# Band attention in a two-block layer: keys of two blocks laid over one another on 128 places, values held as weights, and its steps in other slots

## The chip, the cores and the metric

One core of a Trainium2 chip runs the whole program in one launch. The metric is the device time in microseconds (us) of one execution, as a median of several runs. Engines are named as the profile names them: PE multiplies matrices, PEld is PE's loading of weights, DVE and ACT work element by element, POOL does a few small powers, and SP issues the transfers (DMA).

## The reference, cut to what matters

The program computes two blocks on 512 tokens of width 1024. The change concerns one part of the second block, an attention in which a query sees its own place and the 127 before it, with a learnt "sink" in every denominator:

```
s = einsum('bnqgrd,bnkgd->bngrqk', qb, kband) / sqrt(64)    # kband: the block before and the own block, 256 keys
valid = (rel >= 0) & (rel < 128) & (kpos >= 0)              # rel = query place - key place
s = where(valid, s, -inf)
m = maximum(max(s, -1), sk)
p = exp(s - m);  p = p / (sum(p, -1) + exp(sk - m))
o = einsum('bngrqk,bnkgd->bnqgrd', p, vband)
o_at = rms_norm(o.reshape(B, S, 512), attn_norm_g)
y = concatenate([h_ml, o_at], -1) @ w_out                   # h_ml: the mLSTM branch
x = x + g1 * rms_norm(y, post_mix_g)
```

There are 4 blocks of 128 queries, 8 query heads of width 64, and 2 key heads that serve 4 query heads each. A query at place q of its block sees the keys k > q of the block before and the keys k <= q of its own block: 128 keys in all, one for every k.

## The kernel before, in words

Every large product is made in three PE passes of a format with half the cost of full float32 (a high and a low part of each operand; the trace names operands hh, hl, whi, wlo). ACT makes the high part of a weight tile (whi), DVE the low part (wlo, line 243), and PE takes them in lines 273 (tile ga), 311 and 351 (gb) and 1480 (go). Smaller products, attention among them, are made in full float32, which PE runs as two instructions for one product.

In the second block's mixer PE goes through sixteen slots of about 24 such products each (`fill_items`: queries and keys of the mLSTM, its values, its output gates). After each slot a string names the steps that are put there (`MIX_SLOTS`): R are rotations of queries and keys, A the attention, M the mLSTM, G its gates, W weights of the output projection. `A23` is step 3 of query block 2. A scheduler then fixes the order of each engine's instructions, and every engine works through its own in that order: a PE instruction that waits holds all that stand behind it. PSUM tiles of the attention come from one ring of four (`PS`, tag "ps").

The attention of one query block (`att_stages`, lines 1295 to 1356) has six steps. Steps 0 and 1, one for each half of the heads: two mask products (line 1306, tile sps) put minus 1e30 at forbidden places of two PSUM tiles, four score products (line 1310) are added, DVE takes the maxima over 256 places (line 1313), ACT takes the exponentials out of PSUM and sums them (line 1322). Steps 2 and 3: PE transposes the 128x256 exponentials of each head in two pieces (line 1334, tile ptps), ACT copies them (line 1336). In step 3 the products with the values follow (line 1343, tile ops): the transposed exponentials are the weights, 64 columns of values move; DVE divides by the denominators (line 1346). Step 4 norms over the 512 features of a token (lines 1350 to 1352). Step 5 transposes the result (line 1362, tile tps) and splits it into high and low (lines 388 and 389, tiles ath and atl), ready to be the weights of the output projection (line 1480). Query block 0 has one key block, so its tiles have 128 places instead of 256.

Of the kernel before, what the change touches and what calls it, by code (L numbers as in the profile page):

```python
# [20 lines left out]
C_ID, C_TRI, C_STR, C_LAST, C_CNT, C_COS, C_SIN, C_NEG, C_ATT = (  # L21
    0, 128, 256, 384, 512, 576, 704, 832, 960)
C_W = 1216
# [3 lines left out]
def hybrid_kernel(  # L27
# [46 lines left out]
    # ---------------------------------------------------------------- constants  # L74
# [7 lines left out]
    def stage(parts):  # L82
        raw = small("colraw", [P, P])
        o = 0
        for a in parts:
            dma(out=raw[o:o + a.shape[0]], in_=a)
            o += a.shape[0]
        return raw, o
# [52 lines left out]
    # ---------------------------------------------------------------- adaLN modulation  # L141
# [3 lines left out]
    def ada_steps(ci, col):  # L145
        """steps that sum the products of the 128-column pieces col and col + 1 of w_ada over their k-tiles."""
# [12 lines left out]
    def ada_sum(ci, col, accs):  # L159
        """the sums over partitions of four pieces, as columns."""  # L160
# [16 lines left out]
    def pump():  # L177
        """half a piece of the modulation for every pump_rate[0] tiles of weights."""
# [32 lines left out]
    def cols_to_dram(name, col):  # L211
        """[P, n] columns -> n rows in DRAM."""
# [9 lines left out]
    def rows_bcast(name, dr, r0):  # L222
        """four rows of 128 from r0 on, the same in every partition."""
# [4 lines left out]
    def cols_to_rows(name, col):  # L228
        """[P, 8] columns -> two [P, 512] tiles with the vector in every row, by way of DRAM."""
# [8 lines left out]
    # ---------------------------------------------------------------- products  # L238
# [7 lines left out]
    def split_w(parts, kt=8):  # L246
        """weights [kt * 128, 256] (in column parts) -> per k-tile (hi, lo)."""
# [29 lines left out]
    def load_b(wmat, cols, k0):  # L277
        """two k-tiles of the columns [(first, number)] of wmat."""
# [8 lines left out]
    def keep(raw):  # L287
        """weights split into tiles that stay."""
# [129 lines left out]
    def h_tile(xh, j, p, ts, gc, bc, on_act=False, bank=PS):  # L418
        """features j of the tokens ts: transposed, scaled, shifted and split into p."""
# [14 lines left out]
    def first_tiles(ws, acts, between=None):  # L434
        """products of the first two 256-column weights, by token halves."""
# [8 lines left out]
    def conv(ps, name, cols, taps, b):  # L444
        """depthwise causal convolution of a [features, tokens] product; cols[k] are [P, 1]."""
# [7 lines left out]
    def silu2(u):  # L453
        """silu(2u), in place."""
# [4 lines left out]
    def log1p_exp_negabs(y, n, name):  # L459
        """log(1 + exp(-|y|)) of [P, n] with the relative accuracy of float32."""  # L460
# [15 lines left out]
    # ================================================================ block 1: mixer  # L476
# [68 lines left out]
    # parameters of the convolution  # L545
# [30 lines left out]
    # time steps: the k-tiles in four column groups of the tensor engine, summed with the transposition  # L576
# [15 lines left out]
    def xbc_items(g):  # L592
        """closures that add the convolved tiles of group g to XBC[g]."""
# [19 lines left out]
    # pool branch  # L613
# [25 lines left out]
    for q in (3, 2, 1, 0):  # L639
# [4 lines left out]
    # remaining parameters  # L644
    colF = columns("colF", stage([rows(a_) for a_ in (
        norm_mlp_w, pre_mix_g_2, pre_ffn_g_2, ssd_norm_w, pool_scale, attn_norm_g_2, post_mix_g_2, post_ffn_g_2)]
        + [ml_norm_g_2[0]]))
# [28 lines left out]
    ones_r = const("ones_r", [P, P], F32R)  # L676
    V.tensor_copy(out=ones_r, in_=ones)
    ident_r = const("ident_r", [P, P], F32R)
    V.tensor_copy(out=ident_r, in_=ident)
    masks = U("masks")[:, 0:3 * P]  # L680
    dma(out=masks, in_=consts[:, C_NEG:C_W])
    masks_r = const("masks_r", [P, 3 * P], F32R)
    V.tensor_copy(out=masks_r, in_=masks)
    neg_r, att_r = masks_r[:, 0:P], masks_r[:, P:]
# [27 lines left out]
    # time steps  # L712
# [47 lines left out]
    # state-space branch, a group of eight heads at a time  # L760
# [3 lines left out]
    def ssd_decay(g, cc, st):  # L764
        """what chunk cc of group g needs besides the state: scaled inputs, decayed scores, decayed C."""
# [54 lines left out]
    def ssd_out(g, cc, st):  # L820
        """the outputs of chunk cc of group g and the state after it."""
# [32 lines left out]
    def rms_stages(tiles, eps, wcol, name, res):  # L854
        """tiles [features, tokens] -> normed over all their features, scaled by wcol, split, added to res."""
# [43 lines left out]
    def branch_items(g):  # L899
        """the groups g - 1 and g."""  # L900
# [35 lines left out]
    def weave(stages, items):  # L936
        """emits the stages with the items [(cost, step)] spread evenly between them."""
# [11 lines left out]
    def take(items, share):  # L949
        """the leading items that make up a share of the cost."""  # L950
# [96 lines left out]
    # ================================================================ block 1: MLP  # L1047
# [95 lines left out]
    # ================================================================ block 2: mixer  # L1143
# [25 lines left out]
    # gates of the mLSTM  # L1169
# [58 lines left out]
    # queries and keys of the mLSTM, values and output gates  # L1228
# [24 lines left out]
    # sliding-window attention  # L1253
# [39 lines left out]
    AT = [None] * NCH  # L1293

    def att_stages(b):
# [4 lines left out]
        mx, nm, es, den = (small(n, [P, 8]) for n in ("amx", "anm", "aes", "aden"))  # L1300
        sm = []
        for hq in range(2):
            pse = [PS("sps") for _ in range(2)]
            p3s = [p_[:, 0:2 * nk].rearrange("p (h k) -> p h k", k=nk) for p_ in pse]
            for p3 in p3s:
                PE.matmul(p3, lhsT=ident_r, rhs=mask, start=True, stop=False)
            for i in range(2):
                hp = hq * 2 + i
                for r_, p3 in enumerate(p3s):
                    PE.matmul(p3[:, i], lhsT=QT[b][r_ * 64:(r_ + 1) * 64, hp * P:(hp + 1) * P],  # L1310
                              rhs=KT[hq][r_ * 64:(r_ + 1) * 64, k0:k0 + nk], start=False, stop=i == 1)
            for r_, p3 in enumerate(p3s):
                V.tensor_reduce(out=mx[:, hq * 4 + r_:hq * 4 + 4:2], in_=p3, axis=AX.X, op=ALU.max)
# [4 lines left out]
            u = [U("sm") for _ in range(2)]  # L1318
            for i in range(2):
                for r_ in range(2):  # L1320
                    h = hq * 4 + i * 2 + r_
                    act(out=u[r_][:, i * nk:(i + 1) * nk], in_=pse[r_][:, i * nk:(i + 1) * nk], func=AF.Exp, scale=0.125,
                        bias=nm[:, h:h + 1], accum_out=den[:, h:h + 1])
                    sm.append(u[r_][:, i * nk:(i + 1) * nk])
            yield
        act(out=es, in_=es, func=AF.Exp)
# [371 lines left out]
```

## Time and profile before

| | us |
|---|---|
| median of 3 runs | 1637.94 (1637.54 to 1638.12) |
| profiled execution: span from first to last instruction | 1635.9 |
| what lies around the span, median less span | 2.0 |
| PE busy in the span | 1605.5 |
| DVE busy in the span | 1069.6 |
| ACT busy in the span | 721.2 |

For the profiled execution the profile gives its span alone; its own time is therefore taken as the span and the 2.0 us. Attention runs from about 1085 us to 1186 us of the span. In lists of instructions a line of the profile gives the kernel's line, the engine, the operation, the tile written, the tiles read, and shapes as partitions x elements. The duration of a PE instruction includes its way through the array, so durations overlap: what one costs is read from start to start, or from the chain of waits, where a piece is counted once.

### The profile page before, as it was taken

Reading aid. Unit: us, or ns where it says so; the run is one execution under the profiler, and the core shown is the slowest. Engines: PE = TensorE matmul, PEld = TensorE weight load, DVE = VectorE, ACT = ScalarE, POOL = GpSimd, SP = SyncE. Lnnn points to the kernel's source line nnn. Section 1 sums busy time; section 2 is a strip of 40 time slices with the busy share of each in tenths; the row PEclk is TensorE's granted clock in tenths of the full one; section 3 lists DMA queues with packets and bytes.
Section 4 is the critical chain, followed back from the end, with each engine's and each line's share of the span. In section 5 each row is a group of like instructions: output and inputs, shape, how many; then the busy total and the mean of one; then the engine's idle time right before and its main releaser. Section 6 shows DMA issues by size and latency. Waiting matters only on the chain.

```text
span 1635.9 us, 21014 instructions
## 1 busy us (share of the span) xinstructions
PE 1605.5 (98%) x7942; PEld 1293.6 (79%) x7942; DVE 1069.6 (65%) x1944; ACT 721.2 (44%) x1279; POOL 28.1 (2%) x46
## 2 busy tenths in 40 slices
PE   5999999999999999999999999999999999999998
PEld 3778777777877878877877788878888888888886
DVE  6686898889676676875267654584576756245644
ACT  3543665555454333533123333646555544144421
POOL 0000000000000000000000000000001000000000
PEclk9999999999999999999999999999999999999999
DMA  9632544454544444565246571132232333332321
GB/s 284 185 104 66 174 142 142 130 160 132 158 129 142 129 140 144 167 201 185 91 143 194 181 242 27 53 93 62 72 105 71 90 91 103 91 103 82 99 90 52
DMA packets 206762, 206.52 MB, mean 126 GB/s; under 512 B 11397, under 2 KB 184645, under 8 KB 206661
## 3 DMA queue, kind: packets, MB, share of 16 engines
q1 hardware_dynamic: 206661, 205.19, 40.6%
q8 instruction: 62, 1.02, 0.3%
q14 instruction: 39, 0.32, 0.1%
HBM read 202.96 MB, written 2.19 MB: 125 GB/s over the span
## 4 chain that ended last, share of the span: by engine, by line
PE 93%; DVE 2%; DMA 2%; ACT 1%; issue 1%; POOL 0%; SPq 0%; DVEq 0%; POOLq 0%; ACTq 0%
PE ga L273 54%; PE gb L351 21%; PE gb L311 5%; PE go L1480 2%; PE ga L543 2%; DMA wraw<-in_w_ada_dram 1%; PE yps L831 1%; PE ops L1343 1%; PE stps L840 1%; PE nps L423 1%; PE sps L1310 1%; PE yps L836 1%; PE adaps L163 0%; PE xtps L792 0%; PE ptps L1334 0%
## 5 line engine op out<-in xcount | busy, mean ns | idle before, releaser
L243 DVE TENSOR_TENSOR wlo<-wraw,whi 128x1024 fp32r<-128x1024 f32 (+3 forms) x249 | 298.0, 1198 | 256.3 <-ACT whi L242 256.0
L273 PE MATMUL ga<-hh,whi 128*128 128x512 f32 (+1 forms) x1200 | 465.2, 390 | 0.3 <-ACT hh L430 0.3
L273 PE MATMUL ga<-hl,whi 128*128 128x512 f32 (+1 forms) x1200 | 459.2, 384 | 3.0 <-DVE hl L432 2.9
L273 PE MATMUL ga<-hh,wlo 128*128 128x512 f32 (+1 forms) x1200 | 458.0, 382 | 0.0
L242 ACT ACTIVATE whi<-wraw 128x1024 fp32r<-128x1024 f32 (+3 forms) x249 | 257.8, 1036 | 341.2 <-PE ga L273 152.1
L273 PEld LDWEIGHTS ga<-hl,whi 128*128 128x128 f32 x1200 | 226.0, 189 | 52.4 <-DVE hl L432 3.9
L273 PEld LDWEIGHTS ga<-hh,whi 128*128 128x128 f32 x1200 | 224.6, 188 | 53.2 <-issue 6.4
L273 PEld LDWEIGHTS ga<-hh,wlo 128*128 128x128 f32 x1200 | 226.1, 189 | 47.1 <-issue 0.3
L156 DVE SCALAR_TENSOR_TENSOR adacc<-wraw,csil,adacc 128x256 f32<-128x256 f32 x280 | 133.6, 482 | 30.9 <-DMA wraw<-in_w_ada_dram 26.4
L351 PE MATMUL gb<-whi,hidh 128*128 128x512 f32 x240 | 78.2, 396 | 0.0
L351 PE MATMUL gb<-wlo,hidh 128*128 128x512 f32 x240 | 77.8, 395 | 0.0
L351 PE MATMUL gb<-whi,hidl 128*128 128x512 f32 x240 | 77.5, 394 | 0.0
L449 DVE SCALAR_TENSOR_TENSOR xs<-xraw,colB,xs 128x511 f32<-128x511 f32 (+2 forms) x72 | 53.9, 748 | 9.1 <-ACT xs L447 8.3
L351 PE MATMUL gb<-whi,fh 128*128 128x512 f32 x176 | 57.1, 395 | 0.0
L351 PE MATMUL gb<-wlo,fh 128*128 128x512 f32 x176 | 57.1, 394 | 0.0
L351 PE MATMUL gb<-whi,fl 128*128 128x512 f32 x176 | 56.9, 393 | 0.0
L351 PEld LDWEIGHTS gb<-whi,hidh 128*128 128x128 f32 x240 | 45.0, 188 | 10.8 <-issue 0.4
L351 PEld LDWEIGHTS gb<-whi,hidl 128*128 128x128 f32 x240 | 45.1, 188 | 10.7
L351 PEld LDWEIGHTS gb<-wlo,hidh 128*128 128x128 f32 x240 | 45.1, 188 | 10.5
L805 ACT ACTIVATE arel<-AB,acs 128x128 f32<-128x128 f32 x128 | 40.7, 389 | 26.8 <-DMA AB<-acs 18.8
L273 PE MATMUL ga<-yh,whi 128*128 128x512 f32 x128 | 51.3, 401 | 0.0
L273 PE MATMUL ga<-yl,whi 128*128 128x512 f32 x128 | 50.5, 394 | 0.0
(417 smaller groups left out, 2398.3 us busy)
## 6 DMA issues: line engine op xcount, KB each, us to landing
wraw<-in_w_ada_dram SPq DMA_DIRECT2D x80, 512.0 KB
wraw<-in_w_in_dram SPq DMA_DIRECT2D x72, 512.0 KB
wraw<-in_w_down_dram SPq DMA_DIRECT2D x54, 512.0 KB
wraw<-in_w_up_dram SPq DMA_DIRECT2D x88, 256.0 KB
wraw<-in_w_up_dram SPq DMA_DIRECT2D x32, 512.0 KB
araw<-in_w_ada_dram SPq DMA_DIRECT2D x32, 256.0 KB
AB<-acs SPq DMA_DIRECT2D x32, 256.0 KB
wraw<-in_w_branch_ssd_dram SPq DMA_DIRECT2D x16, 512.0 KB
```

What stands on the lines that cost most here:

```text
L156: V.scalar_tensor_tensor(out=acc, in0=raw[:, k], scalar=s_, in1=acc, op0=ALU.mult, op1=ALU.add)
L242: act(out=hi, in_=raw, func=AF.Copy)
L243: V.tensor_tensor(out=lo, in0=raw, in1=f(hi), op=ALU.subtract)
L273: PE.matmul(ps[:, n0:n1], lhsT=a[:, m * P:(m + 1) * P], rhs=b[:, n0:n1], start=i == 0, stop=i == 3 * n - 1)
L311: PE.matmul(pss[t][:, 0:ncols], lhsT=a[:, t * P:(t + 1) * P], rhs=b, start=k == 0 and j == 0, stop=k == n - 1 and j == 2)
L351: PE.matmul(pss[t][q], lhsT=a, rhs=w[b][q], start=i == 0 and j == 0, stop=i == n - 1 and j == 2)
L423: PE.transpose(ps[:, i * P:(i + 1) * P], xh[t][j // 4][:, (j % 4) * P:(j % 4 + 1) * P], ident)
L449: V.scalar_tensor_tensor(out=o[:, d:], in0=ps[:, 0:S - d], scalar=cols[taps - 1 - d], in1=o[:, d:], op0=ALU.mult, op1=ALU.add)
L543: PE.matmul(fps[i], lhsT=a[:, i * P:(i + 1) * P], rhs=b, start=j == 0 and q == 0, stop=j == 7 and q == 2)
L805: act(out=t[:, i * P:(i + 1) * P], in_=AB[q][:, i * P:(i + 1) * P], func=AF.Relu, scale=-1.0, bias=acs[:, hh:hh + 1])
L831: PE.matmul(ps[r * 64:(r + 1) * 64, j * P:(j + 1) * P], lhsT=xdt[:, hh * 64:(hh + 1) * 64], rhs=M[hh // 4][:, (hh % 4) * P:(hh % 4 + 1) * ...
L1480: PE.matmul(opss[t][q], lhsT=x_, rhs=w[q][b_], start=half == 0 and k == 0 and j == 0, stop=half == 1 and k == 3 and j == 2)
```

## The change

- The scores of the two key blocks are laid over one another. ACT copies the 128 places of the own block from PSUM (a `Copy` of 128 x 2 x 128), and DVE overwrites the places k > q with those of the block before (`copy_predicated`; in block 0 with minus 1e30). Mask products and their constants go.
- Maxima, exponentials and transposes then have 128 places a head. Exponentials are taken in place, out of SBUF.
- A denominator is added up and inverted for each half of the heads, and DVE multiplies the exponentials by it ahead of the transposition. The transposed tile is written twice, once with the places k <= q and once with k > q kept.
- The values are the weights: two products of 64 columns wide weights with 512 moving columns for each key block, the two key heads in the two halves of the PE array. What comes out already has features in partitions, so step 5's transposes go, and high and low are split straight out of PSUM.
- The norm of the attention is not applied to its output. Its factor per token (`att_r`, one POOL power) is taken from a product with ones (tile assps); the mLSTM half is multiplied by the factor's inverse (`att_ri`), and the factor comes back in `post`, two small DVE operations more for each token tile.
- The rows of the attention's half of `w_out` and its gains are loaded in another order (two transfers of 64 rows for each tile of 128).
- The steps stand in other slots. Comments and docstrings are gone, which moves line numbers.

The core of the diff:

```diff
     def att_stages(b):
+        nk = 2 * P if b else P
         k0 = (b - 1) * P if b else 0
-        nk = 2 * P if b else P
-        kb = nk // P
-        mask = (att_r if b else att_r[:, P:]).unsqueeze(1).to_broadcast([P, 2, nk])
...
             p3s = [p_[:, 0:2 * nk].rearrange("p (h k) -> p h k", k=nk) for p_ in pse]
-            for p3 in p3s:
-                PE.matmul(p3, lhsT=ident_r, rhs=mask, start=True, stop=False)
             for i in range(2):
                 hp = hq * 2 + i
                 for r_, p3 in enumerate(p3s):
                     PE.matmul(p3[:, i], lhsT=QT[b][r_ * 64:(r_ + 1) * 64, hp * P:(hp + 1) * P],
-                              rhs=KT[hq][r_ * 64:(r_ + 1) * 64, k0:k0 + nk], start=False, stop=i == 1)
+                              rhs=KT[hq][r_ * 64:(r_ + 1) * 64, k0:k0 + nk], start=i == 0, stop=i == 1)
+            u = U("sm")
+            sm.append(u)
+            c4 = u.rearrange("p (i r k) -> p i r k", r=2, k=P)
             for r_, p3 in enumerate(p3s):
-                V.tensor_reduce(out=mx[:, hq * 4 + r_:hq * 4 + 4:2], in_=p3, axis=AX.X, op=ALU.max)
+                act(out=c4[:, :, r_], in_=p3[:, :, nk - P:nk], func=AF.Copy)
+                V.copy_predicated(out=c4[:, :, r_], mask=up2,
+                                  data=p3[:, :, 0:P] if b else never.unsqueeze(1).to_broadcast([P, 2, P]))
...
+            V.tensor_reduce(out=mx[:, h4], in_=h3(u), axis=AX.X, op=ALU.max)
...
-            for i in range(2):
-                for r_ in range(2):
-                    h = hq * 4 + i * 2 + r_
-                    act(out=u[r_][:, i * nk:(i + 1) * nk], in_=pse[r_][:, i * nk:(i + 1) * nk], func=AF.Exp, scale=0.125,
-                        bias=nm[:, h:h + 1], accum_out=den[:, h:h + 1])
+            for j in range(4):
+                h = hq * 4 + j
+                act(out=u[:, j * P:(j + 1) * P], in_=u[:, j * P:(j + 1) * P], func=AF.Exp, scale=0.125,
+                    bias=nm[:, h:h + 1], accum_out=den[:, h:h + 1])
+            act(out=es[:, h4], in_=es[:, h4], func=AF.Exp)
             yield
...
-        for hp in range(4):
+        for g in range(2):
+            h4 = slice(g * 4, g * 4 + 4)
+            V.tensor_tensor(out=den[:, h4], in0=den[:, h4], in1=es[:, h4], op=ALU.add)
+            V.reciprocal(out=den[:, h4], in_=den[:, h4])
+            V.tensor_tensor(out=h3(sm[g]), in0=h3(sm[g]), in1=den[:, g * 4:g * 4 + 4].unsqueeze(2).to_broadcast([P, 4, P]),
+                            op=ALU.mult)
             ps = PS("ptps")
-            for i in range(2 * kb):
-                o = i % kb * P
-                PE.transpose(ps[:, i * P:(i + 1) * P], sm[hp * 2 + i // kb][:, o:o + P], ident)
-            t_ = U("pT")
-            act(out=t_[:, 0:2 * nk], in_=ps[:, 0:2 * nk], func=AF.Copy)
+            for j in range(4):
+                PE.transpose(ps[:, j * P:(j + 1) * P], sm[g][:, j * P:(j + 1) * P], ident)
+            t_ = [U("pT") for _ in range(2 if b else 1)]
+            V.tensor_tensor(out=h3(t_[0]), in0=h3(ps), in1=tri.unsqueeze(1).to_broadcast([P, 4, P]), op=ALU.mult)
+            if b:
+                V.tensor_tensor(out=h3(t_[1]), in0=h3(ps), in1=strict.unsqueeze(1).to_broadcast([P, 4, P]), op=ALU.mult)
             pT.append(t_)
...
-        for h in range(8):
-            for i in range(kb):
-                PE.matmul(ps[:, h * 64:(h + 1) * 64], lhsT=pT[h // 2][:, (h % 2 * kb + i) * P:(h % 2 * kb + i + 1) * P],
-                          rhs=kv[b - kb + 1 + i][:, 128 + h // 4 * 64:128 + (h // 4 + 1) * 64], start=i == 0, stop=i == kb - 1)
-        oa = U("oa")
-        V.tensor_tensor(out=hd(oa), in0=hd(ps), in1=den.unsqueeze(2).to_broadcast([P, 8, 64]), op=ALU.mult)
...
+        for i in range(len(pT[0])):
+            for g in range(2):
+                PE.matmul(ps[g * 64:(g + 1) * 64], lhsT=kv[b - i][:, 128 + g * 64:128 + (g + 1) * 64], rhs=pT[g][i],
+                          start=i == 0, stop=i == len(pT[0]) - 1)
+        sq = U("asq")
+        act(out=sq, in_=ps, func=AF.Square)
         AT[b] = pair("at")
-        token_cols(oa, AT[b])
+        split(ps, AT[b])
+        V.tensor_tensor(out=sq[:, 0:2 * P], in0=sq[:, 0:2 * P], in1=sq[:, 2 * P:], op=ALU.add)
+        s1 = small("asq1", [P, P])
+        V.tensor_tensor(out=s1, in0=sq[:, 0:P], in1=sq[:, P:2 * P], op=ALU.add)
+        yield
+        ps = PS("assps")
+        PE.matmul(ps[:, 0:1], lhsT=s1, rhs=ones[:, 0:1], start=True, stop=True)
...
-        V.tensor_tensor(out=dn, in0=dn, in1=r, op=ALU.mult)
+        V.scalar_tensor_tensor(out=dn, in0=dn, scalar=att_ri[cc], in1=r, op0=ALU.mult, op1=ALU.mult)
...
+        if fac is not None:
+            V.scalar_tensor_tensor(out=s1, in0=s1, scalar=fac, in1=fac, op0=ALU.mult, op1=ALU.mult)
         r = rsqrt(s1, D, 1e-6, "n")
+        if fac is not None:
+            V.tensor_tensor(out=r, in0=r, in1=fac, op=ALU.mult)
...
-MIX_SLOTS = ("", "R11 G1 R02 R12 A00 A01", "R20 G2 G3 A02 A10 R21", "A11 A03 A12 R22", "A04 A13 R30", "A05 A20 A21",
...
+MIX_SLOTS = ("", "R11 G1 R02 R12 A00", "R20 G2 A01 R21", "G3 A02 A10 R22", "A03 A11", "A04 A12 R30",
```

What the scheduler makes of it, on PE, where the scores of query block 1 stand. A row is the kernel's line, the operation, the tile written and the tiles read (sps scores, kT and qT keys and queries, ptps transposed exponentials, qtps transposed queries, ga and gb large products); x4 are four in a row. Before:

```order
L215 MATMUL rowps<-consts,bm 16x128
L1334 MATMUL ptps<-consts,sm 128x128 x4
L1306 MATMUL sps<-masks_r,ident_r 128x512
L1310 MATMUL sps<-kT,qT 128x256 x2
L273 MATMUL ga<-hl,whi 128x512
L1306 MATMUL sps<-masks_r,ident_r 128x512
L1310 MATMUL sps<-kT,qT 128x256 x2
L273 MATMUL ga<-hh,wlo 128x512
```

And now:

```order
L312 MATMUL gb<-whi,hh 128x512
L1337 MATMUL ptps<-consts,sm 128x128 x4
L1308 MATMUL sps<-kT,qT 128x256 x4
L1281 MATMUL qtps<-consts,qo 128x128 x4
L312 MATMUL gb<-wlo,hh 128x512
L312 MATMUL gb<-whi,hl 128x512
```

The mask products are gone, and the four score products of a half stand together; before, those of one half of block 1 and of one of block 2 stood two and two with other products between.

On PE, where the products with the values stand (ops, read from pT and kv). Before, those of query block 0 and the first of block 1:

```order
L1343 MATMUL ops<-kv,pT 128x64 x4
L1334 MATMUL ptps<-consts,sm 128x128 x2
L1343 MATMUL ops<-kv,pT 128x64 x2
L1334 MATMUL ptps<-consts,sm 128x128
L1343 MATMUL ops<-kv,pT 128x64 x2
L1334 MATMUL ptps<-consts,sm 128x128 x5
L1283 MATMUL qtps<-consts,qo 128x128 x4
L1288 MATMUL ktps<-consts,ko 128x128 x2
L1334 MATMUL ptps<-consts,sm 128x128 x8
L1343 MATMUL ops<-kv,pT 128x64 x8
```

And now, those of query block 0:

```order
L312 MATMUL gb<-wlo,hh 128x512
L1337 MATMUL ptps<-consts,sm 128x128 x4
L1308 MATMUL sps<-kT,qT 128x256 x4
L312 MATMUL gb<-whi,hl 128x512
L1347 MATMUL ops<-pT,kv 64x512 x2
L312 MATMUL gb<-whi,hh 128x512
```

Eight products of 64 columns have become two of 512 with half the array each; transposes are four at a time instead of eight.

On DVE, between the scores of a half and the next step of the mLSTM's keys (sm exponentials, amx maxima, aden denominators, qk the convolution of the mLSTM's keys). Only now:

```order
L1315 COPY_PREDICATED sm<-consts,sps 128x2x128 x2
L1318 TENSOR_REDUCE amx<-sm 128x4
L1319 SCALAR_TENSOR_TENSOR anm<-amx,sink 128x4
L1320 TENSOR_TENSOR aes<-sink,anm 128x4
L1321 TENSOR_SCALAR anm<-anm 128x4
L1360 TENSOR_SCALAR attv_10010<-assps 128x1
L1364 TENSOR_TENSOR atti_10014<-attv_10010,attr_10012 128x1
L1331 TENSOR_TENSOR aden<-aden,aes 128x4
L1332 RECIPROCAL aden<-aden 128x4
L1333 TENSOR_TENSOR sm<-sm,aden 128x512
L450 SCALAR_TENSOR_TENSOR qk<-qkraw,colC,qk 128x511
```

Before, the same stretch of DVE held two reductions and three small operations for a half; the copies, the scaling and, behind the transposes, the two products with the triangles are new there.

## Rows read from the trace of the kernel before

**Rows 1.** The page: span, busy time by engine, and the chain that ended last.
```profile
span 1635.9 us, 21014 instructions
PE 1605.5 (98%) x7942; PEld 1293.6 (79%) x7942; DVE 1069.6 (65%) x1944; ACT 721.2 (44%) x1279; POOL 28.1 (2%) x46
...
PE 93%; DVE 2%; DMA 2%; ACT 1%; issue 1%; POOL 0%; SPq 0%; DVEq 0%; POOLq 0%; ACTq 0%
```
**Rows 2.** Attention's stretch: length, busy PE, PEld, DVE, ACT, POOL (x instructions), clock, DMA.
```profile
1086.00:1183.00 97.00, 96.99 (x536) 78.35 (x537) 55.69 (x129) 55.46 (x142) 2.20 (x4) 1.00 0.21 62
```
**Rows 3.** Chain of waits from 1075 to 1275 us: shares, then pieces (start, us, what).
```profile
by line: PE ga L273 23.8%; PE gb L311 22.8%; PE go L1480 19.6%; PE ops L1343 6.0%; PE sps L1310 4.9%; PE ptps L1334 3.1%; PE sps L1306 1.9%; PE tps L1362 1.8%; PE mops L1414 1.8%; PE mscps L1379 1.8%; PE nps L423 1.5%; PE cps L1397 1.5%; PE
...
1086.40 0.65 PE sps L1310 x8
...
1092.31 1.06 PE sps L1310 x4
...
1119.17 1.06 PE sps L1310 x8
...
1135.24 0.87 PE ptps L1334 x8
1136.11 3.52 PE ops L1343 x32
```
**Rows 4.** PE in order of time: start, duration, line, tiles; two separate stretches.
```profile
68.30 1.06 PE L583 MATMUL ga<-hh,wraw 128*32 128x512 f32 x8
69.18 1.04 PE L583 MATMUL ga<-hl,wraw 128*32 128x512 f32 x8
...
304.75 0.39 PE L836 MATMUL yps<-EC,st 128*64 128x128 f32 x4
304.97 0.39 PE L831 MATMUL yps<-arel,xdt 128*64 128x128 f32 x4
```
**Rows 5.** PE in order of time, where float32 products stand between large ones.
```profile
1100.71 0.40 PE L311 MATMUL gb<-whi,hl 128*128 128x512 f32 x1
1100.94 0.63 PE L1306 MATMUL sps<-masks_r,ident_r 128*128 128x512 f32 x2
1101.50 1.14 PE L1310 MATMUL sps<-kT,qT 64*128 64x256 f32 x8
1102.56 0.50 PE L311 MATMUL gb<-whi,hh 128*128 128x512 f32 x1
1102.90 0.39 PE L311 MATMUL gb<-wlo,hh 128*128 128x512 f32 x1
```
**Rows 6.** DVE groups from 1083 to 1202 us: us in total, mean ns, idle before them.
```profile
L243 DVE TENSOR_TENSOR wlo<-wraw,whi 128x1024 fp32r<-128x1024 f32 x9 | 11.0, 1222 | 6.3 <-ACT whi L242 6.3
L1313 DVE TENSOR_REDUCE amx<-sps 128x2 f32<-128x512 f32 x12 | 8.1, 688 | 2.0 <-PE sps L1310 2.0
L1346 DVE TENSOR_TENSOR oa<-ops,aden 128x512 f32<-128x512 f32 x4 | 2.8, 692 | 8.0 <-PE ops L1343 8.0
L1190 DVE TENSOR_TENSOR_SCAN MT<-FT,LS 4x512 f32<-4x512 f32 x1 | 1.2, 1211 | 0.0
```
**Rows 7.** DVE in order of time: 256 columns, and two small operations in a chain.
```profile
1100.39 0.42 DVE L1272 TENSOR_TENSOR qo<-rc,rs 128x256 f32<-128x256 f32 x1
...
1253.94 0.15 DVE L1496 TENSOR_TENSOR ns<-nss 128x1 f32<-128x1 f32 x1
1254.12 0.15 DVE L393 TENSOR_SCALAR nv<-ns 128x1 f32<-128x1 f32 x1
```
**Rows 8.** Waits of PE and PEld, 1040 to 1275 us: total, times, longest.
```profile
PE ga L273 <- DVE hl L432: 0.3, 1, 0.3
...
PEld mtps L1194 <- ACT sm L1322: 0.4, 1, 0.4
PEld ptps L1334 <- ACT sm L1322: 0.3, 1, 0.3
...
PEld ops L1343 <- ACT sm L1322: 0.2, 1, 0.2
```

More of the change, by code (lines that the diff above doesn't have):

```diff
@@ L85, in stage @@
         for a in parts:
-            dma(out=raw[o:o + a.shape[0]], in_=a)
+            dst = raw[o:o + a.shape[0]]
+            dma(out=dst if len(a.shape) == 2 else dst.rearrange("p (e d) -> p e d", d=a.shape[-1]), in_=a)
             o += a.shape[0]
@@ L645, in hybrid_kernel @@
     colF = columns("colF", stage([rows(a_) for a_ in (
-        norm_mlp_w, pre_mix_g_2, pre_ffn_g_2, ssd_norm_w, pool_scale, attn_norm_g_2, post_mix_g_2, post_ffn_g_2)]
-        + [ml_norm_g_2[0]]))
+        norm_mlp_w, pre_mix_g_2, pre_ffn_g_2, ssd_norm_w, pool_scale)]
+        + [attn_norm_g_2.rearrange("o (e j d) -> (o j) e d", e=2, d=64)]
+        + [rows(a_) for a_ in (post_mix_g_2, post_ffn_g_2)] + [ml_norm_g_2[0]]))
     nf_col, pm_col, pf_col = colF[:, 0:8], colF[:, 8:16], colF[:, 16:24]
@@ L675, in hybrid_kernel @@
     V.tensor_copy(out=dsk_col[64:128], in_=dsk_row[64:128].rearrange("p (j r) -> p j r", r=2)[:, :, 1])
[L676 to L684, printed above, removed]
+    neg = const("neg", [P, P])
+    dma(out=neg, in_=consts[:, C_NEG:C_W])
+    never = const("never", [P, 1])
+    G.memset(never, NEG)
+    upper = K[:, C_UP:C_UP + P].bitcast(mybir.dt.int32)
     GP = []
@@ L1347, in att_stages @@
-        yield
-        j_ = U("njunk")
-        ss = small("ass", [P, 1])
-        act(out=j_, in_=oa, func=AF.Square, accum_out=ss)
-        r = rsqrt(ss, 512, 1e-6, "n")
-        act(out=oa, in_=oa, func=AF.Copy, scale=r)
-        yield
-        AT[b] = pair("at")
-        token_cols(oa, AT[b])
+        for i in range(len(pT[0])):
+            for g in range(2):
+                PE.matmul(ps[g * 64:(g + 1) * 64], lhsT=kv[b - i][:, 128 + g * 64:128 + (g + 1) * 64], rhs=pT[g][i],
+                          start=i == 0, stop=i == len(pT[0]) - 1)
@@ new lines, in att_stages @@
+        sq = U("asq")
+        act(out=sq, in_=ps, func=AF.Square)
+        AT[b] = pair("at")
+        split(ps, AT[b])
+        V.tensor_tensor(out=sq[:, 0:2 * P], in0=sq[:, 0:2 * P], in1=sq[:, 2 * P:], op=ALU.add)
+        s1 = small("asq1", [P, P])
+        V.tensor_tensor(out=s1, in0=sq[:, 0:P], in1=sq[:, P:2 * P], op=ALU.add)
+        yield
+        ps = PS("assps")
+        PE.matmul(ps[:, 0:1], lhsT=s1, rhs=ones[:, 0:1], start=True, stop=True)
+        v = const("attv%d" % b, [P, 1])
+        V.tensor_scalar(out=v, in0=ps[:, 0:1], scalar1=1.0 / 512, scalar2=1e-6, op0=ALU.mult, op1=ALU.add)
@@ L1356, in att_stages @@
+        att_r[b] = const("attr%d" % b, [P, 1])
+        G.tensor_tensor(out=att_r[b], in0=v, in1=mhalf[:, 0:1], op=ALU.pow)
+        att_ri[b] = const("atti%d" % b, [P, 1])
+        V.tensor_tensor(out=att_ri[b], in0=v, in1=att_r[b], op=ALU.mult)
         yield
@@ L1450, in load_wo @@
         raw = RAW([P, 1024])
-        dma(out=raw, in_=wo2[k * P:(k + 1) * P, :])
+        if k < 4:
+            dma(out=raw, in_=wo2[k * P:(k + 1) * P, :])
+        else:
+            for e in range(2):
+                r0 = 512 + e * 256 + (k - 4) * 64
+                dma(out=raw[e * 64:(e + 1) * 64], in_=wo2[r0:r0 + 64, :])
         col = mln_col[:, k:k + 1] if k < 4 else attn_col[:, k - 4:k - 3]
@@ L1481, in out_mm, with post @@
                               stop=half == 1 and k == 3 and j == 2)
-    def post(src, t, GG, before=None):
+    def post(src, t, GG, before=None, fac=None):
         y = []
@@ L1552, in front2 @@
     def front2(t):
-        post(opss, t, G1)
+        post(opss, t, G1, None, att_r[t])
         yield
@@ L1668, in shape_constants @@
     k[:, C_NEG:C_NEG + P] = np.where(r[None, :] < r[:, None], NEG, 0.0)
-    k[:, C_ATT:C_ATT + P] = np.where(r[None, :] > r[:, None], 0.0, NEG)
-    k[:, C_ATT + P:C_ATT + 2 * P] = np.where(r[None, :] <= r[:, None], 0.0, NEG)
+    k[:, C_UP:C_UP + P] = r[None, :] > r[:, None]
     for q in range(4):
```

20 lines of the change are left out of this document (8 added, 12 removed).

## Prediction

> **What bounds the kernel now.** I read the page first, then the stretch in which attention stands, then the chain of waits there, and last what DVE has to do. The page shows PE busy for 98% of the span, and 93% of the chain that ended last is PE [rows 1]. In the stretch from 1086 to 1183 us PE is busy for 96.99 of 97 us at the full clock (1.00, its level of 2.4 GHz), DVE for 55.69 and ACT for 55.46 [rows 2]. The chain of waits runs through PE alone there, so attention costs what its PE pieces cost [rows 3]. Therefore the sum is one of PE instructions, and then one asks whether DVE, which gets more to do, still delivers in time.
>
> The sum is made against the profiled execution: 1635.9 us of span and 2.0 us around it, together the median of 1637.94 us [rows 1]. The 2.0 us are left as they are.
>
> **The change part by part, on PE.** The chain's by-line row covers 200 us (1075 to 1275), so 1% is 2.0 us [rows 3]. Attention before: value products (line 1343) 6.0%, 12.0 us; scores (1310) 4.9%, 9.8 us; transposes of the exponentials (1334) 3.1%, 6.2 us; masks (1306) 1.9%, 3.8 us; line 1362 1.8%, 3.6 us, of which half, 1.8 us, is the attention's (16 transposes of 32). Together 33.6 us.
>
> *Value products.* Before there are 7 key blocks times 8 heads, 56 products, each two PE instructions: 112. Thirty-two take 3.52 us, 0.11 us each although only 64 columns move [rows 3]; PE pays there for loading 128 columns of weights. Now there are 14 products of 512 columns, 28 instructions. Eight instructions of 512 columns that use four quarters of the array take 0.86 to 0.88 us from start to start [rows 4], so one alone would take 4 x 0.87 / 8 = 0.43 us. Four instructions in two halves of the array take 0.22 us for 128 columns [rows 4], 0.055 each, half of what a full-array float32 instruction takes (0.11). So halves run side by side, and one instruction costs 0.43 / 2 = 0.215 us: 28 x 0.215 = 6.0 us. Gain 6.0 us. Bounds: 0 if the halves ran one behind the other (28 x 0.43 = 12.0 us), and 6.0.
>
> *Scores.* Their number stays. A half of a query block takes 1.06 us when its eight instructions stand together, and 1.06 us for four of them when it is split [rows 3]. Two halves were split, and none of those is now (one of block 0 is, at 0.65 us a half; I leave it). Gain 2 x 1.06 = 2.1 us.
>
> *Transposes.* Eight take 0.87 us, 0.11 each [rows 3]. 56 become 32, and the 16 of the result go: 24 x 0.11 + 1.8 = 4.4 us. *Masks* go: 3.8 us.
>
> *Added:* four products with ones, eight instructions that load 128 columns of weights; the nearest row is the 0.11 us of the value products, so 0.9 us. Sum: 6.0 + 2.1 + 4.4 + 3.8 - 0.9 = 15.4 us less.
>
> *Fewer changes between kinds of products.* Behind float32 products the first large one takes 0.34 us to the next start (1102.56 to 1102.90) where 0.23 is usual (1100.71 to 1100.94) [rows 5]: 0.11 us. By the new order float32 groups between large products go from 30 to 23 in this part of the program: 7 x 0.11 = 0.8 us less.
>
> The Trainium skill speaks against the change here. Its page TensorEngine Tiling (Array Packing), section Key Properties, says that changing the tiling mode, not merely the tile, drains the engine. The 0.34 us behind the row-tiled scores agree with that [rows 5]. Each of the four groups of value products is now column-tiled, and three of them stand next to row-tiled or full-array float32 work, where nothing was switched before. At 0.11 us for one to two switches a group that is 0.4 to 0.9 us; by the rule the sum would be about 1626.5 us instead of 1625.9. I leave it out, since it lies within what I put down for waits below.
>
> **On DVE and ACT.** Removed from DVE: 12 maxima of 512 places at 0.688 and 4 smaller ones (9.9 us), 4 divisions at 0.692 (2.8 us). Added: 8 maxima at 0.688 (5.5), 8 scalings at 0.692 (5.5), 14 products with a triangle at 0.692 (9.7), 4 sums of 256 and 4 of 128 columns (about 2.8), 24 small operations at 0.15 to 0.18 where 12 go, net about 2.2 [rows 6, 7]. The trace has no predicated copy. A 256-column operation takes 0.42 us [rows 7]; the slowest operation on 512 columns, the scan, takes 1.21 us, so 0.6 for 256 [rows 6]; at twice the speed of the former it would be 0.21. Sixteen cost between 3.4 and 9.7 us; I take 0.42, the nearest row, 6.7 us. Net: 32.4 - 12.7 = 19.7 us more. ACT loses the copies of the transposed tiles, the scaling and half of each exponential, and gains sixteen copies; it ends lower and is not looked at further.
>
> PE's stretch of 97 us becomes about 82, and DVE's work in it 55.7 + 19.7 = 75.4: 92% instead of 57%. The cover of DVE's work is thus nearly used up. PE now meets attention's DVE results at sixteen places: eight groups of transposes, four of value products, four products with ones. Behind a waiting PE instruction stand all large products of the next slot. The trace of before has three waits of this kind, 0.4, 0.3 and 0.2 us [rows 8]. A place can cost from nothing to one weight split, 1.22 us, the longest operation that can stand in front on DVE [rows 6]: 0 to 19.5 us in all. I take the mean of the three, 0.3, for each: 4.8 us, less the 0.9 us that were there, 3.9 us more. PSUM has a part in it: a pair of score tiles is free when DVE's copies have read it, no longer when ACT's exponentials have.
>
> **Behind the mixer.** `post` has two small DVE operations more in a chain, 0.18 us from one start to the next [rows 7]: 0.4 us for a token tile. PE waits 0.3 us there already for DVE's hl [rows 8], so one of the four is seen: 0.4 us. The other three lie beside the output projection. Weights in two transfers of 64 rows are asked for slots ahead; I put nothing down. If that cover were gone it would be one landing.
>
> Sum: -15.4 - 0.8 + 3.9 + 0.4 = -11.9 us. 1637.9 - 11.9 = 1626.0 us.
>
> **The rivals.**
> *DVE sets the pace.* For it: 92% leaves 7 us of idle time in 82, while DVE had 41 idle of 97 because it waits for ACT and PE in its own order [rows 2]. Against: the weights' low parts are made several slots ahead, so only attention itself would wait. If DVE gets no further than 85%, the stretch is 75.4 / 0.85 = 89 us, 8 less than 97; with 0.8 gained and 0.4 lost, 1630 us; at 80%, 94 us and 1634. The Trainium skill's page TensorEngine Tiling (Array Packing), section PSUM Bottleneck, has the rule: tiling speeds TensorE up and leaves the evacuation of PSUM as it is, which may then bound.
> *The halves do not run side by side*, so the change doesn't do what it says in the value products: 6.0 us come back, 1632 us. Against: both pairs of rows above [rows 4].
> *Slower.* The ring of four PSUM tiles. A half's pair of score tiles stays taken until ACT's copy and DVE's predicated copy have come up in their own orders, and PE, which needs the ring for the next half or the next transposes, stands still. At eight halves this decides from (15.4 + 0.8 - 0.4) / 8 = 2.0 us a half. A weight split and two 512-column operations in front of the copies are 1.22 + 2 x 0.69 = 2.6 us; with 8 x 2.6 = 20.8 us the time is 1637.9 - 15.8 + 20.8 = 1643 us. Against: the new order puts the copies directly ahead of the maxima, and the halves lie a slot of some 5.6 us (24 x 0.23) apart.
>
> **How the numbers follow.** The forecast, with waits between 0 and 8 us, 1621 to 1629 us: 0.69. DVE sets the pace, 1629 to 1635: 0.18. Halves in turn: 0.04. Slower by the ring: 0.05; the last 0.04 lie within 0.2%, in between. The range reaches from a little below no waits (1637.9 - 16.2 - 0.9 = 1620.8) to DVE at 80%: 1620.5 to 1634. About 0.2%, 3.3 us, is what a measurement of this kernel can tell from no change. Faster 0.91, same 0.04, slower 0.05.
>
> **What would show it.** In the new profile: the value products 28 instructions, starts 0.2 us apart; scores eight in a row in 1.06 us; no mask products; 32 transposes. DVE near 90% in the stretch and a few waits of PE for DVE (sm, pT) or for the ring, each under a microsecond. Wrong would be: value products 0.43 us apart; waits of PE for DVE above 8 us in all, which is the second case; or score products that wait for predicated copies, which is the last. A predicated copy of over 0.6 us would make the DVE sum wrong.

## The result and the profile after

| | before | changed |
|---|---|---|
| median, measured beside each other | 1637.74 us (1636.68 to 1638.12, 4 runs) | 1624.55 us (1624.03 to 1625.33, 4 runs) |
| ratio | | 0.992, 95% interval 0.9908 to 0.9932 |
| span of the profiled execution | 1635.9 us | 1622.3 us |

The forecast was 1626.0 us in a range from 1620.5 to 1634. The page of the changed kernel, against [rows 1]: PE still fills the span, DVE has 16.9 us more.
```profile
span 1622.3 us, 20792 instructions
PE 1589.5 (98%) x7810; PEld 1274.0 (79%) x7810; DVE 1086.5 (67%) x1995; ACT 715.4 (44%) x1275; POOL 28.3 (2%) x47
```
The stretch of attention that [rows 2] shows holds 257 large products in 97 us; 256 of them now take 83 us (block 3's value products lie just behind it). In the windows (length, busy PE, PEld, DVE, ACT, POOL, clock, DMA) PE loses 0.42 us of it, and DVE is at 87%, not at the 92% of the forecast:
```profile
1086.00:1169.00 83.00, 82.58 (x414) 61.70 (x413) 71.89 (x177) 50.48 (x140) 1.84 (x3) 1.00 0.25 69
```
The chain of waits (start, us, what) shows pieces that answer to [rows 3]. Transposes come four at a time, a half's eight score instructions stand together at 1.06 us, and eight value product instructions take 1.87 us, 0.23 each:
```profile
1100.50 0.44 PE ptps L1337 x4
1100.94 1.06 PE sps L1308 x8
...
1108.14 1.01 PE ops L1347 x4
...
1128.25 0.44 PE ktps L1286 x2
...
1146.27 1.87 PE ops L1347 x8
```
Among DVE's groups of this stretch (us in total, mean ns, idle before), those that answer to [rows 6], with the operation that the trace of before did not have. The predicated copy (DVE's overwriting of the places k > q) takes 0.44 us, and 0.50 where its data is one number for each partition:
```profile
L1333 DVE TENSOR_TENSOR sm<-sm,aden 128x512 f32<-128x512 f32 x8 | 5.5, 690 | 0.2
L1339 DVE TENSOR_TENSOR pT<-ptps,consts 128x512 f32<-128x512 f32 x8 | 5.5, 684 | 0.0
L1318 DVE TENSOR_REDUCE amx<-sm 128x4 f32<-128x512 f32 x8 | 5.5, 682 | 0.1
L1315 DVE COPY_PREDICATED sm<-consts,sps 128x256 f32<-128x256 int32 x12 | 4.7, 442 | 0.1
...
L1315 DVE COPY_PREDICATED_SCALAR sm<-consts,never 128x256 f32 x4 | 1.8, 496 | 0.0
```
All waits of PE from 1083 to 1262 us (total, times, longest), against [rows 8]. Only the last stands in attention, before the transposes of rotated keys (ktps); the first lies behind the mixer, the second in the output projection:
```profile
PE ga L274 <- ACT hh L431: 0.6, 1, 0.6
PE ips L1430 <- DVE mod L171: 0.6, 1, 0.6
PE ktps L1286 <- DVE atl L390: 0.4, 1, 0.4
```
To compare executions I use three intervals between starts in PE's order of time: *attention*, from the first gate transposition (tile gfps) to the first output product (go), as in the changed kernel
```profile
1083.00 0.49 PE L1184 MATMUL gfps<-consts,lf 128*4 128x128 f32 x3
...
1188.27 0.50 PE L1494 MATMUL go<-whi,ath 128*128 128x512 f32 x1
```
then the *projection* to the last token tile's first pair of nps transposes, and the *entry* to the last group of them.

| us | before | changed | difference |
|---|---|---|---|
| up to attention | 1082.88 | 1083.00 | + 0.12 |
| attention | 119.20 | 105.27 | - 13.93 |
| projection | 54.94 | 55.77 | + 0.83 |
| entry | 14.03 | 14.26 | + 0.23 |
| the rest of the span | 364.85 | 364.00 | - 0.85 |

On PE the change touches nothing in the first and the last line.

### The profile page after: what moved, and what is told of

It reads as the page before. It is cut to its first block, busy times and chain, and to the rows that moved or that the text cites. A ratio compares the mean times of both kernels' runs of the same rounds, so it can differ in the third digit from the quotient of the medians.

```text
span 1622.3 us, 20792 instructions
## 1 busy us (share of the span) xinstructions
PE 1589.5 (98%) x7810; PEld 1274.0 (79%) x7810; DVE 1086.5 (67%) x1995; ACT 715.4 (44%) x1275; POOL 28.3 (2%) x47
## 4 chain that ended last, share of the span: by engine, by line
PE 90%; DVE 4%; DMA 3%; ACT 2%; issue 1%; SPq 0%; POOL 0%; DVEq 0%; POOLq 0%; ACTq 0%
PE ga L274 53%; PE gb L352 21%; PE gb L312 5%; PE go L1494 2%; PE ga L544 2%; DMA wraw<-in_w_ada_dram 1%; DMA AB<-acs 1%; DVE wlo L244 1%; PE nps L424 1%; PE yps L829 1%; PE stps L838 0%; ACT arel L803 0%; PE yps L834 0%; DMA x<-in_x_dram 0%; PE adaps L164 0%
## 5 line engine op out<-in xcount | busy, mean ns | idle before, releaser
L274 PE MATMUL ga<-yh,wlo 128*128 128x512 f32 x128 | 50.6, 395 | 0.0
```

The lines of the kernel that those rows point to most:

```text
L274: PE.matmul(ps[:, n0:n1], lhsT=a[:, m * P:(m + 1) * P], rhs=b[:, n0:n1], start=i == 0, stop=i == 3 * n - 1)
```

## Experiments

The kernel before had a median of 1637.3 to 1638.5 us beside these runs. The same instructions outside attention can take 1 to 2 us more or less in another execution, so attention's interval in each trace is read beside the medians.

**The changed kernel again.** 

> The changed kernel once more, on the same chip as the next three, so that these can be set against it: 1624 to 1627 us.


1623.88 us, ratio 0.9913 (0.9899 to 0.9926); attention 105.20.

**Table or form: each alone.** One kernel has the new code and the old table (its edit is shown), the other the old code and the new table.
```
-MIX_SLOTS = ("", "R11 G1 R02 R12 A00", "R20 G2 A01 R21", "G3 A02 A10 R22", "A03 A11", ...
+MIX_SLOTS = ("", "R11 G1 R02 R12 A00 A01", "R20 G2 G3 A02 A10 R21", "A11 A03 A12 R22", "A04 A13 R30", ...
```

> The changed kernel with the table of slots of the kernel before. My theory: the gain is in the TensorE instructions that the new form leaves out, and the table moves little: 1623 to 1629 us, at most some 4 us of waits more than with the new table (1624.6), since five of the places where TensorE meets attention's results then stand closer together. Rival: the new table carries the gain, by keeping waits small: 1631 to 1638 us.

> The kernel before with the new table of slots alone. My theory: no TensorE instruction goes, so 1636 to 1641 us, the same or a little slower than before (1637.7). Rival, that the new table carries the gain: 1626 to 1633 us.


New form, old table: 1636.2 us, ratio 0.9993 (0.9984 to 1.0002), attention 115.85. Old form, new table: 1639.63, ratio 1.0007 (0.9998 to 1.0016), attention 120.49. So by the medians neither alone is told from no change, and both together give 13 us. In attention's interval the new form alone gains 3.4 us and the new table alone loses 1.3. My theory of the first fell. With the old table PE waits before transposes and before the rotated keys' transposes (ktps):
```profile
PE ptps L1337 <- DVE sm L1333: 3.3, 2, 2.4
PE ktps L1286 <- DVE aden L1332: 2.8, 1, 2.8
```
In order of time (the wait in brackets), two of these stalls follow one another, and the windows show the granted clock at 0.50, 1.2 GHz, from 1131.25 to 1137.50 us:
```profile
1127.90 0.39 PE L312 MATMUL gb<-whi,hl 128*128 128x512 f32 x1
1130.73 0.72 PE L1337 MATMUL ptps<-consts,sm 128*128 128x128 f32 x4 [2.44 <-DVE sm L1333]
1131.25 1.06 PE L1281 MATMUL qtps<-consts,qo 128*128 128x128 f32 x4
1135.07 0.66 PE L1286 MATMUL ktps<-consts,ko 128*128 128x128 f32 x2 [2.77 <-DVE aden L1332]
```
```profile
1131.25:1137.50 6.25, 3.48 (x14) 2.68 (x13) 4.26 (x16) 3.60 (x8) 0.00 (x0) 0.50 0.28 84
```
PE worked 3.48 us at half clock there, which by an estimate costs 1.7. With 6.1 us of waits and 2.0 us more for value products (8.6 for 6.6) that is 9.8 of the 10.6 us. The remaining 0.8 us are scores (8.84 for 8.08), since one half is split again:
```profile
1121.63 1.06 PE sps L1308 x4
...
1123.11 1.06 PE sps L1308 x4
```
DVE was busy for 4.26 of the 6.25 us: it was not full, its results came late.

**Do the halves work side by side?** First the order of the value products, then a load on one half alone:
```
-        for i in range(len(pT[0])):
-            for g in range(2):
+        for g in range(2):
+            for i in range(len(pT[0])):
```

> The changed kernel; the value products of one column half stand all ahead of those of the other, where now the halves alternate. The same 28 instructions, in another order. My theory (the halves run side by side, one instruction alone takes 0.43 us): in blocks 1 to 3 eight instructions go from 1.87 us to 7 x 0.43 = 3.0 us, block 0 stays: + 3.4 us, 1628 us. Rival, that an instruction takes its 0.23 us by itself and the halves don't overlap: no change, 1624.6 us.

```
+        for _ in range(3):
+            for i in range(len(pT[0])):
+                PE.matmul(ps[0:64], lhsT=kv[b - i][:, 128:192], rhs=pT[0][i], ...)
```

> The changed kernel; the value products of the lower column half are issued three more times (the same result again), so that in blocks 1 to 3 sixteen instructions go to one half and four to the other, and in block 0 eight and two. If a half takes 0.43 us for an instruction and the two halves work side by side, each with a queue of its own (which would explain that the order half by half took no longer), a block's products take 16 x 0.43 = 6.9 us, block 0's 3.4: in all + 17 us, about 1642. If an instruction on half the columns takes 0.23 us by itself, whichever half, 20 x 0.23 = 4.6 and 2.3 us: + 9.5 us, about 1634.

Half by half: 1626.77 us, ratio 0.9929 (0.9916 to 0.9941), attention 105.20, and a group still takes 1.87 us in the chain:
```profile
1146.36 1.87 PE ops L1347 x8
```
One half four times: 1645.24 us, ratio 1.0045 (1.0031 to 1.0058), attention 125.12; the four groups' added work is 18.0 us of it. The twelve added instructions of one half take 5.16 us, 0.43 each:
```profile
1130.01 5.16 PE ops L1351 x12
```
So an instruction takes 0.43 us, two halves with work share that time, and it does not matter in which order the two halves' products stand, if they stand together. (A large product's pass over 512 columns takes 0.23 us. A float32 product is two instructions, so such a pass costs about a quarter of it, or half of one instruction.) My expectation of the first run fell on that; the second excludes its rival. The Trainium skill, page TensorEngine Tiling (Array Packing), section Key Properties, says that tiles work independently of one another; the two runs agree.

**More work for DVE.**
```
-                V.copy_predicated(out=c4[:, :, r_], mask=up2, ...)
+                for _ in range(2):
+                    V.copy_predicated(out=c4[:, :, r_], mask=up2, ...)
```

> The changed kernel with each of the 16 predicated copies issued twice, 12 x 0.44 + 4 x 0.49 = 7.2 us more on VectorE, and each pair of score tiles in PSUM held up to 0.9 us longer. My theory (TensorE sets the pace and VectorE has 11 us left in the 83 us of attention): 1624.5 to 1626.5 us. Rival, VectorE sets the pace at 87%: the whole 7 us come out, 1631 to 1632 us, with waits for sm and pT. Second rival, the ring of four PSUM tiles: about 8 x 0.9 = 7 us too, but as waits of score products and transposes for a tile.

1628.11 us, ratio 0.9939 (0.9925 to 0.9952), attention 106.11: 0.84 us more in the stretch where the copies are, with two waits of 0.4 and 0.6 us:
```profile
PE assps L1359 <- DVE asq L1356: 0.6, 1, 0.6
...
PE ptps L1338 <- DVE sm L1334: 0.4, 1, 0.4
```
The copies' groups take 12.0 us instead of 6.5, and nothing near the rivals' 7 us shows in attention. The window over attention:
```profile
1084.32:1190.43 106.11, 105.11 (x552) 80.13 (x551) 91.14 (x228) 61.81 (x164) 2.81 (x4) 1.00 0.28 80
```
Most of the 4 us in the span lies outside attention, where no instruction differs. It is no chance of one execution, for all five took 1627.6 us or more; its cause stays open. The edit is also not quite alone: the scheduler put the transposes at other places, 57, 69, 35, 43, 25, 71, 25 and 70 large products behind their scores, where the changed kernel has 51, 63, 23, 39, 34, 48, 48 and 48. So the run shows that DVE's load does not set the pace of attention, and not what longer copies cost in the same order.

**How far apart: transposes nearer to their scores.**
```
+MIX_SLOTS = (..., "R20 G2 A01 A02 R21", "G3 A03 A10 R22", "A11 A12", "A04 A13 R30", "A05 A20 R31", "A14 A21 A22 R32", ...
```

> The changed kernel with the transposes of most halves one slot nearer to their scores and the value products one later. Between a half's scores and its transposes then lie 42, 59, 26, 33, 17, 34, 30, 43 large products (now 51, 63, 23, 39, 34, 48, 48, 48; with the old table 43, 43, 14, 57, 13, 11, 45, 72). New theory: what TensorE waits for is the length of the chain from scores to scaled exponentials (copies, maximum, exponentials, denominator, scaling), about 6.4 us in the run with the old table, so it waits where less than that, some 25 products, lies between: here at the one place with 17, for 1 to 3 us, 1626 to 1628 where the changed kernel takes 1625. Rival, that VectorE's whole load or the ring of PSUM tiles makes the waits: none here, 1625, or waits at many places, over 1629.

1627.71 us, ratio 0.9938 (0.9924 to 0.9952), attention 107.96. The time came out as I had said and the reason did not: PE waited 0.34 us behind 26 products and 0.48 behind 30, not behind 17, where another wait of 0.53 us came first. No one distance decides. The trace also has the clock at 0.50 from 1090 to 1093 us, which by an estimate makes some 1.7 of the 2.7 us, ahead of the places that the edit moves. So most of the time that I had forecast came from elsewhere, and the number was luck.

**The old table with block 1 later, and then the rotation too.**
```
+MIX_SLOTS = (..., "R20 G2 G3 A02 R21", "A03 A10 R22", "A04 A11 R30", "A05 A12 A20 A21", "A13 A22 R31 R32", "A14 A23 A24 A30", ...
```

> The changed kernel with the old table, in which only the steps of query block 1 stand where the new table has them (each one to two slots later). Between a half's scores and its transposes then lie 43, 56, 35, 30, 22, 22, 48, 72 large products, where the old table gave 43, 43, 14, 57, 13, 11, 45, 72; the second transposes of blocks 2 and 3 stay directly ahead of their value products. In the run with the old table (1636.2 us) TensorE stood still 0.85 and 2.44 us before transposes and 2.77 us for a PSUM tile, between 1105 and 1137 us, and its clock fell to half from 1131 to 1137.5 us, which makes some 2 us more. My theory, that the distance from scores to transposes decides: these go, and 6 to 9 us come back, 1627 to 1630 us. Rival, that the old table is slower for some other reason (value products right behind the transposes, block 0 or block 3): 1633 to 1636 us.

1634.42 us, ratio 0.9982 (0.9973 to 0.9991), attention 113.12. The two waits before transposes went (0.3 us is left), but the larger wait stayed, and grew. DVE's order of time shows what the transposes of the keys waited for: the rotated keys (ko) stand behind block 1's triangle products and a weight split. The clock fell again behind the stall (last row, a window).
```profile
1126.00 0.68 DVE L1341 TENSOR_TENSOR pT<-ptps,consts 128x512 f32<-128x512 f32 x1
...
1127.07 1.22 DVE L244 TENSOR_TENSOR wlo<-wraw,whi 128x1024 fp32r<-128x1024 f32 x1
...
1128.61 0.22 DVE L1270 TENSOR_TENSOR ko<-rc,rs 128x64 f32<-128x64 f32 x1
```
```profile
1128.98 0.66 PE L1286 MATMUL ktps<-consts,ko 128*128 128x128 f32 x2 [3.19 <-DVE aden L1332]
...
1129.00:1132.25 3.25, 3.25 (x10) 1.01 (x10) 0.69 (x3) 1.92 (x5) 0.00 (x0) 0.50 0.54 161
```
The edit that follows from it, on top of that kernel:
```
-"A05 A12 A20 A21", "A13 A22 R31 R32"
+"A05 A12 A20 A21 R31", "A13 A22 R32"
```

> The kernel of the run before last (old table, block 1 later, 1634.4 us), and besides the second step of block 3's rotation (VectorE rotates the keys) one slot earlier than their transposes, as the new table has it; the old one has both in one slot. In that run TensorE stood still for 3.2 us before those transposes (1125.8 to 1129.0 us), while VectorE had the products with the triangles and a weight's low part ahead of the rotation, and the clock was at half until 1132.3 us, which makes 1.7 us more. Theory: the transposes waited for the rotated keys, in VectorE's order: 4 to 5 us come back, 1629 to 1631 us. Rival, the ring of four PSUM tiles (the transposes take the fourth tile behind a half's scores): 1633 to 1635 us.

1630.54 us, ratio 0.9956 (0.9943 to 0.9968), attention 108.78, 4.3 us back: the wait and the fall of the clock are gone. Of the 3.5 us that still part it from the new table, 2.1 are value products (8.75 us for 6.61): the scheduler puts large products between the two halves' instructions, and the two instructions of one product alone take 1.00 us. Scores cost 1.6 us more (9.70 for 8.08), in part because one half is split.
```profile
1160.02 1.00 PE ops L1347 x2
...
1165.86 1.01 PE ops L1347 x4
...
1167.54 1.00 PE ops L1347 x2
```
**The same step moved back in the new table.**
```
-"A05 A13 A20 R31", "A14 A21 R32"
+"A05 A13 A20", "A14 A21 R31 R32"
```

> The changed kernel with this one step moved back: block 3's keys are rotated in the slot of their transposes, not one ahead. The distances from scores to transposes and from transposes to value products stay as they are (51, 63, 23, 39, 34, 48, 48, 48 and 1, 10, 24, 24 large products). Theory (VectorE's order decides, not its load): the transposes come some 2 to 3 us late, and with the clock perhaps 1 to 2 more: 1626.5 to 1629 us. Rival: TensorE finds them ready as before, since nothing but one slot of 5.6 us is given up: 1624 to 1625 us.

1625.15 us, ratio 0.9926 (0.9913 to 0.994), attention 105.36. The rival was right: the scheduler put five more large products ahead of these transposes, and PE waited 0.5 us. One slot is not what decides. That it is what else stands there on DVE is what the lists of the two runs before suggest; no run tests it alone.

**A shorter chain under the old table.** The sums with the sinks, the reciprocals and the scaling are left out, so the probabilities stay undivided.
```
-            V.tensor_tensor(out=den[:, h4], in0=den[:, h4], in1=es[:, h4], op=ALU.add)
-            V.reciprocal(out=den[:, h4], in_=den[:, h4])
-            V.tensor_tensor(out=h3(sm[g]), in0=h3(sm[g]), in1=..., op=ALU.mult)
```

> The changed kernel with the old table, and without the sums with the sinks, the reciprocals and the scaling of the exponentials (the probabilities are left undivided): 24 VectorE operations less, 8 x (0.17 + 0.18 + 0.69) = 8.3 us, and the chain from scores to transposes shorter by about 1.2 us with its steps between engines. If the length of that chain makes the waits of the old table: the two waits before transposes lose 0.85 and 1.2 us or more, 1631 to 1634 us. Rival, that the ring of PSUM tiles and the order of blocks make them: 1635 to 1637 us, as with the scaling.

1630.15 us, ratio 0.9958 (0.9946 to 0.9971), attention 109.77: 6.1 us less than with the scaling, and no wait of PE in attention above 0.2 us. That speaks for the chain, but DVE's load fell with it, and the scheduler made another order on PE (some transposes stand singly between large products). The three are not told apart here.

**Two waits moved.** `R32` ahead of `A14 A21`; the mLSTM's norm in two steps, the first one slot earlier.

> The changed kernel with two moves against its two remaining waits: the transposes of the last rotation stand ahead of block 1's value products, so that their PSUM tile is not the one of those products (0.55 us lost there), and the first half of the mLSTM's norm for chunk 0 stands a slot earlier, so that the modulation's evacuation is not queued behind it (0.6 to 0.8 us lost). My theory: 0.8 to 1.4 us less than the changed kernel on this chip. Rival: the next tile or evacuation is as late, no change.

1627.66 us, ratio 0.9936 (0.9924 to 0.9949): not faster than the changed kernel (1623.88 beside it). The projection lost 0.34 us as meant (55.43), attention has 107.43, with 9.4 us of scores for 8.1 and, as the windows show, half the clock for 3.25 us in which PE was busy all the time. That makes by an estimate 1.6 of its 2.2 us, so what the moved transposes are worth is not seen:
```profile
1089.25:1092.50 3.25, 3.25 (x12) 2.53 (x10) 3.25 (x13) 0.96 (x1) 0.00 (x0) 0.50 0.00 0
```
None of the versions beats the changed kernel.

## Why the prediction was right, step by step

PE bounds attention, and with the new table the sum of its instructions carries the result. By starts in PE's order of time, in attention's interval (predicted, measured):

| us | predicted | measured |
|---|---|---|
| value products, 12.0 before | - 6.0 | - 5.3 (11.87 to 6.61) |
| scores and masks | - 5.9 | - 6.4 (14.49 to 8.08) |
| transposes | - 4.4 | - 3.8 (7.61 to 3.77) |
| products with ones | + 0.9 | + 0.55 |
| changes between kinds of products | - 0.8 | + 0.2 |
| waits of PE for DVE and its queue, attention | + 3.9 | + 0.55 |
| projection, in which PE waits 0.6 | none | + 0.83 |
| `post` | + 0.4 | + 0.23 |

*Value products.* 0.23 us an instruction where I had 0.215, and block 0's four take 1.01. That the halves share the time is shown, and with it the rival of halves in turn is out.

*Changes between kinds.* Before, the first large product behind a float32 group comes about 0.09 us late at nearly every such place; the excess of the large products over 0.2325 us each is 2.7 us in all. After, it is 3.5 us: 0.55 is the wait at 1128 us, 0.49 stands in front of the four groups of value products (0.20, 0.09, 0.10, 0.10; of the first, 0.10 belongs to the scores ahead of it), and 2.4 is left. So I gained 0.3 instead of 0.8, and lost the 0.4 to 0.5 that I had left out. My count was the mistake: in attention's interval float32 groups with a large product behind them go from 25 to 23, not from 30 to 23. The Trainium skill, page TensorEngine Tiling (Array Packing), section Key Properties, has a change of tiling mode drain the engine; the trace agrees, at the lower end of the 0.4 to 0.9 us that I had put beside it: every column-tiled group loses 0.09 us in front of it, where most full-array float32 groups lose nothing. It is not all a matter of mode, since behind full-array float32 groups the next large product comes 0.08 us late too, for 0.11 behind tiled ones.

*Waits: the term that was mis-sized.* "I take the mean of the three, 0.3, for each: 4.8 us, less the 0.9 us that were there, 3.9 us more." None of the sixteen places waits longer than 0.1 us. The one wait of attention, 0.55 us with what the large product ahead loses, stands at a seventeenth: the transposes of rotated keys, which take the PSUM tile that DVE was still splitting. The price was misread too: the 0.4, 0.3 and 0.2 us of [rows 8] are waits of weight loads for ACT, and PE, busy for 96.99 of 97 us, felt none of them. I gave every place the same price and let the table of slots count only for split scores and changes, 2.9 us. The runs show it the other way round: with the new table the places cost next to nothing, with the old one waits, clock and parted products cost 10.6 us (115.85 for 105.27). The projection's wait, for an evacuation behind the mLSTM's norm on DVE, I had not looked for. I had put 3.4 us too much on the waits in attention, and the other rows together came out 2.1 us dearer than forecast. That these partly cancel (- 13.2 against - 11.9) is luck: of a table that decides over the whole gain the prediction says little.

*DVE.* + 16.9 us of busy time instead of + 19.7, 87% instead of 92%. The durations alone rose by 21.0 us, but operations that follow one another overlap: 0.69 us of duration is 0.60 from start to start (1119.65 to 1120.25 us, two products with the triangles). DVE does not set the pace: with the copies doubled attention grew by 0.84 us. The first rival is out for this table.

*The slower case.* Score tiles did not hold PE up. The nearest thing is the wait at 1128 us, for a tile that DVE still had to split.

*Behind the mixer.* The two operations cost 0.23 us.

What stays open: what lowers the clock at 1089 to 1093 us in three of the runs, where PE had been busy throughout, and why unchanged parts differ by 1 to 2 us from one execution or kernel to another.

## What to carry to other kernels

Where PE sets the pace, count its instructions first; but a form that lengthens the chain between two PE steps on other engines may earn its gain only if other PE work stands between them (here 10.6 of attention's 13.9 us hung on the order), so price form and order together, and try each alone. Ask at each place what stands ahead of the needed result in the other engine's order, not how busy that engine is. Products that share the array by halves have to stand together in the final order: a product of two instructions took 1.00 us apart and 0.47 together.

## What the hardware showed that I had not expected

- Four instructions for one column half ahead of four for the other took the same 1.87 us as alternating ones, so a half's products can wait while those behind them start in the other half.
- A stall can cost twice: behind waits of 2.44 and 3.19 us in attention the granted clock stood at 0.50 for 6.25 and 3.25 us. The changed kernel, whose waits there are 0.6 us at most, shows 1.00 throughout attention.
- The length of a wait alone did not tell whether the clock would fall. All fourteen traces have a wait of 1.8 to 2.7 us near 662 us, in a part that the change leaves alone; behind it the clock fell to 0.50 in six of them and stayed at 1.00 in eight (it fell behind 1.99 us in one, and not behind 2.32 in another). The kernel before and the changed one, each with the wait and the window behind it:
```profile
661.04 0.58 PE L273 MATMUL ga<-hl,whi 128*128 128x256 f32 x1 [2.62 <-DVE hl L432]
661.00:663.75 2.75, 2.71 (x12) 2.71 (x13) 2.75 (x6) 0.93 (x3) 0.00 (x0) 0.50 0.38 132
...
661.57 0.39 PE L274 MATMUL ga<-hl,whi 128*128 128x256 f32 x1 [2.13 <-DVE hl L433]
661.50:665.00 3.50, 2.87 (x22) 2.63 (x22) 3.50 (x10) 1.66 (x5) 0.00 (x0) 1.00 0.38 130
```
